# A two-layer decoder trunk on one core: index work of the expert layers split along the up tiles, low parts moved to VectorE, modulation loads moved

## The chip, the cores and the metric

The kernel runs on one core of one Trainium2 chip. The metric is the device time in microseconds (us) of one execution, the median of several runs. The engines are TensorE (PE in the rows; its weight loads are PEld), VectorE (DVE), ScalarE (ACT), GpSimd (POOL) and SyncE (SP), whose queue starts nearly all DMA transfers. Each engine works through its own instructions in the order in which they stand.

## What is computed

One sequence of 256 tokens with 1024 features passes two layers. The first mixes tokens by retention, the second by sparse attention; each ends with a PEER expert layer. The reference, cut to the expert layer and the modulation:

```python
mod = (c_act @ ada_w[layer] + ada_b[layer])          # shift, scale and gate, twice
h = x * (1.0 + sc2) + sh2
q = (xc @ w_q).reshape(T, PEER_HEADS, 2, PEER_QDIM // 2)
s = jnp.einsum('thcd,hcnd->thcn', q, sub_keys)
sv, si = lax.top_k(s, PEER_TOPK)                     # 16 of 128, two halves, 8 heads
comb = (sv[:, :, 0, :, None] + sv[:, :, 1, None, :]).reshape(T, PEER_HEADS, 256)
cv, ci = lax.top_k(comb, PEER_TOPK)                  # the largest sums
i1 = jnp.take_along_axis(si[:, :, 0], ci // PEER_TOPK, axis=-1)
i2 = jnp.take_along_axis(si[:, :, 1], ci % PEER_TOPK, axis=-1)
w = jax.nn.softmax(cv, axis=-1)
u = u_tab[i1 * PEER_NKEYS + i2]
a = jax.nn.gelu(jnp.einsum('td,thkd->thk', xc, u)) * w
y = jnp.einsum('thk,thkd->td', a, v_tab[i1 * PEER_NKEYS + i2])
```

The kernel does not gather experts. It computes all 16384 products with `u_tab`, multiplies them by a weight matrix W that is zero except at the chosen experts, and multiplies the result with all of `v_tab`.

## The kernel before

**Split numbers.** A float32 matmul is made of three faster ones (`mm3`, lines 120 to 122): both operands are split into a high part and the remainder, the low part. A loaded weight tile `raw` (128x1024, 512 KB, five buffers) is split in two halves of 128x512: ACT copies the high part (`hi`, line 96), and DVE or POOL subtracts for the low part (`lo`, line 103); four buffers each. In `split(raw, lo)` a letter per half names the engine: "d" is DVE, "p" is POOL. Activations are split likewise by `modulate`: ACT scales into `tmp` (line 165), DVE copies `hh` (line 98), DVE or POOL subtracts `hl` (line 103).

**Order.** PE runs in the order of the program text (`manual_schedule`). The other engines are ordered by a scheduler that keeps dependences and may pull an instruction ahead, except inside blocks marked with `WORKERS`.

**First stage** (retention's queries and keys). For each of eight slabs k, `prepare` multiplies two tiles of modulation weights with the conditioning row on DVE (line 301), forms the coefficients (lines 305, 306) and modulates `xT`; then two tiles `ret_qk` are split and 48 matmuls run. The block is marked, so all engines follow the text.

**Background modulation.** `ada_steps` is a generator: one step loads a tile of modulation weights, the next multiplies it on DVE with a row sum (line 140). `drain(bg, n)` takes n steps at chosen places: in the expert layers' loops, in `columns` and between the attention's units. A chunk is eight tiles, 16 steps.

**Expert layer** (`peer`, once per layer). After the queries, `first` takes the 16 largest of 128 for each head and half (lines 562 to 566). `second(tt)`, for each of two token tiles, builds 80 candidate sums (579 to 583), takes the 16 largest of each head (586 to 590), turns their places into two ranks (592 to 605) and looks up the indices by comparison and a tree of additions (608 to 613). Then 60 up tiles follow (`up`, 24 matmuls each, a gelu per pair at line 685). After up tile 15 `weights` takes the softmax (618 to 625), ahead of up tile 20, after tile 19, `finish` transposes indices and weights on PE, and from there `dense` builds W in 34 steps until tile 58 (`DENSE`, `UPLO` and `FINISH` hold these numbers; of the first half's tiles, 18 have their low parts on POOL). Then `down` tiles run, and the second half of experts repeats without index work. All of the index work is on DVE.

**Attention** (`nsa`). `columns` projects keys and queries tile by tile and takes three background steps ahead of each tile; `hidden` reads four `cmp_w1` tiles; `values` follows; then 16 units (`scores`, `turn`, `weighted`) of a head pair and a raw branch each, with two background steps in the first seven.

## Time and profile before

| | us |
|---|---|
| median of 3 runs | 2143.55 (2143.01 to 2144.36) |
| profiled execution, its time | 2146.44 |
| profiled execution, first to last instruction (span) | 2144.7 |
| PE, DVE, ACT, POOL busy | 2029.4, 1663.5, 1207.9, 315.4 |
| mean granted clock of TensorE, share of full | 0.977 |

All rows below are of the profiled execution, whose own time is 2.89 us above the median. Times in rows start at the first instruction. PE is busy for most of the span, so what is to be read are the stretches in which it is not, and the stretches in which its granted clock is under 1.00.

### The profile page before, as it was taken

How to read it: one execution, taken by the hardware profiler on the slowest of the kernel's cores; microseconds unless marked ns; L12 is line 12 of the kernel's file. 1: busy time of each engine (PE TensorE's matmuls, PEld its weight loads, DVE VectorE, ACT ScalarE, POOL GpSimd, SP SyncE). 2: the span in 40 equal slices, each digit the busy share in tenths (PEclk: the TensorE clock that was granted, in tenths of full speed). 3: DMA queues.
4: the chain of work that ended last, by engine and by line, in shares of the span. 5: the costliest groups of instructions: out<-in, count | busy, mean ns of one | idle time of the engine just before them, and what ended most of it. 6: DMA issues, size and time to landing. Idle time of an engine off the chain costs nothing.

```text
span 2144.7 us, 39749 instructions
## 1 busy us (share of the span) xinstructions
PE 2029.4 (95%) x14658; PEld 1820.6 (85%) x14658; DVE 1663.5 (78%) x3705; ACT 1207.9 (56%) x2141; POOL 315.4 (15%) x288
## 2 busy tenths in 40 slices
PE   6899996999999999999978999969999999999997
PEld 6788896999777999978868769969987889998885
DVE  7897589889876778886685766988897667779666
ACT  3455553666555666655542655546755556665554
POOL 3511485000000000000040237800000000000000
PEclk9999998999999999999989999989999999999999
DMA  8787553556777766786657426535567665556664
GB/s 302 244 296 235 187 162 122 161 158 187 232 228 236 220 207 206 219 251 216 195 175 266 168 70 187 160 119 163 165 208 228 188 185 165 166 170 213 194 187 138
DMA packets 116467, 417.06 MB, mean 194 GB/s; under 512 B 13072, under 2 KB 14640, under 8 KB 115376
## 3 DMA queue, kind: packets, MB, share of 16 engines
q1 hardware_dynamic: 115264, 411.90, 61.7%
q8 instruction: 114, 1.87, 0.4%
q10 hardware_dynamic: 1008, 2.63, 0.3%
q14 instruction: 81, 0.66, 0.1%
HBM read 411.31 MB, written 3.16 MB: 193 GB/s over the span
## 4 chain that ended last, share of the span: by engine, by line
PE 77%; DVE 14%; DMA 5%; issue 2%; POOL 1%; ACT 1%; SPq 0%; DVEq 0%; ACTq 0%; POOLq 0%
PE mm L120 12%; PE mm L122 12%; PE mm L121 12%; PE acc L122 11%; PE acc L121 11%; PE acc L120 11%; PE aux L664 3%; DVE lo L103 2%; DMA raw<-in_ada_w 2%; DVE big L612 1%; DVE raw L140 1%; ACT hi L96 1%; DVE big L610 1%; PE aux L982 1%; DMA raw<-in_kv_ada_w 1%
## 5 line engine op out<-in xcount | busy, mean ns | idle before, releaser
L96 ACT ACTIVATE hi<-raw 128x512 fp32r<-128x512 f32 x1272 | 797.0, 632 | 769.3 <-PE acc L122 345.2
L103 DVE TENSOR_TENSOR lo<-raw,hi 128x512 fp32r<-128x512 f32 x1108 | 772.8, 707 | 318.9 <-ACT hi L96 314.2
L120 PE MATMUL mm<-hh,hi 128*128 128x256 f32 x2528 | 730.7, 289 | 18.7 <-ACT hi L96 18.7
L122 PE MATMUL mm<-hh,lo 128*128 128x256 f32 x2528 | 718.1, 284 | 21.1 <-DVE lo L103 19.5
L121 PE MATMUL mm<-hl,hi 128*128 128x256 f32 x2528 | 715.4, 283 | 0.1
L122 PEld LDWEIGHTS mm<-hh,lo 128*128 128x128 f32 x2528 | 480.7, 190 | 24.3 <-DVE lo L103 20.9
L120 PEld LDWEIGHTS mm<-hh,hi 128*128 128x128 f32 x2528 | 481.7, 191 | 20.2 <-ACT hi L96 19.6
L121 PEld LDWEIGHTS mm<-hl,hi 128*128 128x128 f32 x2528 | 481.7, 191 | 1.1 <-POOL hl L103 0.3
L122 PE MATMUL acc<-hi,a 128*128 128x512 f32 x992 | 393.7, 397 | 3.7 <-DVE a L103 3.6
L121 PE MATMUL acc<-lo,a 128*128 128x512 f32 x992 | 392.9, 396 | 0.6 <-DVE lo L103 0.6
L120 PE MATMUL acc<-hi,a 128*128 128x512 f32 x992 | 392.3, 395 | 0.0
L103 POOL TENSOR_TENSOR lo<-raw,hi 128x512 fp32r<-128x512 f32 x164 | 228.4, 1409 | 920.2 <-ACT hi L96 914.4
L122 PEld LDWEIGHTS acc<-hi,a 128*128 128x128 f32 x992 | 186.4, 188 | 54.0 <-DVE a L103 9.1
L121 PEld LDWEIGHTS acc<-lo,a 128*128 128x128 f32 x992 | 186.4, 188 | 47.2 <-DVE lo L103 3.3
L120 PEld LDWEIGHTS acc<-hi,a 128*128 128x128 f32 x992 | 186.5, 188 | 43.4 <-issue 0.2
L140 DVE SCALAR_TENSOR_TENSOR raw<-raw,crow 128x1024 f32<-128x1024 f32 x96 | 121.5, 1270 | 58.7 <-DMA raw<-in_ada_w 46.8
L666 ACT ACTIVATE W<-aux 128x512 f32<-128x512 f32 x128 | 142.7, 1115 | 0.0
L269 POOL TENSOR_TENSOR x<-x,row 128x512 f32<-128x512 f32 x2 | 2.8, 1390 | 736.0 <-ACT x L268 736.0
L103 DVE TENSOR_TENSOR a<-g,a 128x256 fp32r<-128x256 f32 x248 | 103.7, 419 | 0.0
L96 ACT ACTIVATE a<-g 128x256 fp32r<-128x256 f32 x248 | 99.6, 403 | 1.8 <-DVE g L693 1.8
L693 DVE TENSOR_TENSOR g<-g,W 128x256 f32<-128x256 f32 x256 | 94.8, 422 | 1.0 <-ACT W L666 0.8
L655 DVE TENSOR_TENSOR hot<-iota,i 128x1024 f16<-128x1024 f16 x128 | 87.6, 685 | 0.0
(267 smaller groups left out, 1991.0 us busy)
## 6 DMA issues: line engine op xcount, KB each, us to landing
raw<-in_peer_u SPq DMA_DIRECT2D x256, 512.0 KB, 3.6
raw<-in_peer_v SPq DMA_DIRECT2D x256, 512.0 KB, 4.1
raw<-in_ada_w SPq DMA_DIRECT2D x96, 512.0 KB, 4.5
raw<-in_ret_in SPq DMA_DIRECT2D x32, 512.0 KB, 5.0
raw<-in_peer_q SPq DMA_DIRECT2D x32, 512.0 KB, 4.2
raw<-in_ret_qk SPq DMA_DIRECT2D x16, 512.0 KB, 5.8
raw<-in_ret_o SPq DMA_DIRECT2D x16, 512.0 KB, 3.7
raw<-in_kv_ada_w SPq DMA_DIRECT2D x16, 512.0 KB, 4.0
```

The lines of the kernel that those rows point to most:

```text
L96: nc.scalar.activation(dst, src, AF.Copy)
L103: (nc.vector if eng == "dve" else nc.gpsimd).tensor_tensor(dst, x, y, op=OP.subtract)
L120: nc.tensor.matmul(ps, sh, mh, start=start, stop=False, skip_group_check=True)
L121: nc.tensor.matmul(ps, sh, ml, start=False, stop=False, skip_group_check=True)
L122: nc.tensor.matmul(ps, sl, mh, start=False, stop=stop, skip_group_check=True)
L140: nc.vector.scalar_tensor_tensor(raw, raw, 1.0, crow, op0=OP.mult, op1=OP.mult, accum_out=mod[:, o + j:o + j + 1])
L610: V.tensor_tensor(o, o, sf[:, tt, c, :, None].to_broadcast([P, 16, 16, 8]), op=OP.mult)
L612: V.tensor_tensor(o[:, 0:n], o[:, 0:n], o[:, n:2 * n], op=OP.add)
L655: V.tensor_tensor(oA, count(0, P), bc(i2, P), op=OP.is_equal)
L664: nc.tensor.matmul(ps[:, t], ohA[n % 2][:, t], ohB[n % 2][:, x, t], start=(x == 0), stop=(x == 1))
L666: nc.scalar.activation(w[:, :, n * TB:n * TB + TB].rearrange("p b t -> p t b"), ps, AF.Copy, scale=1.0 / WSCALE)
L693: V.tensor_tensor(gi, gi, W[half][:, i % HALF], op=OP.mult)
```

## The change

Four edits, in one file. A constant is added ahead of everything, so a line of the changed kernel is one or more higher than the same line before (103 is 104, 966 is 985).

1. `second` ends after the largest sums. What followed is a generator, `ranks`, in 18 pieces for both token tiles, drawn between up tiles 5 and 18. `weights` comes after tile 9, its second part (`normalised`) after tile 19, `finish` after tile 20, `dense` from 21. Only eight up tiles have their low parts on POOL; from the ninth on they are DVE's.
2. In the first stage all low parts are DVE's; ACT makes the copy `hh`, but for slab 0.
3. `columns` takes no background steps. The attention's units take three steps each in the first eight and two in the next five.
4. One chunk of the second layer's modulation moves from the attention to the first expert layer's background; the down loop of the first half takes a step at each eighth tile more.

```diff
-UPLO = (["pp"] * 18 + ["dd"] * 42, ["dd"] * 60)
-DENSE = (20, 58), (0, 56)
-FINISH = (15, 19)
+UPLO = (["pp"] * 8 + ["dd"] * 52, ["dd"] * 60)
+DENSE = (21, 58), (0, 56)
+FINISH = (9, 20)
+RANKS = (5, 18)
...
-    def modulate(s, h, k, x, lo=None):
+    def modulate(s, h, k, x, lo=None, hi="dve"):
         nc.scalar.activation(t, x, AF.Identity, scale=cA[:, s, k:k + 1], bias=cB[:, s, k:k + 1])
-        copy_to("dve", h[0][:, k], t)
+        copy_to(hi, h[0][:, k], t)
...
-                modulate(0, h1, k, xT[:, k], "dve")
+                modulate(0, h1, k, xT[:, k], "dve", "act" if k else "dve")
...
-                            w[c] = split(load(a["ret_qk"][k, c]), lo="pd")
+                            w[c] = split(load(a["ret_qk"][k, c]), lo="dd")
...
+
+            def ranks(tt):
+
                 for c in range(2):
                     V.tensor_copy(sf[:, tt, c], si[:, tt, :, c].rearrange("p h j -> p j h"))
 
...
                 V.tensor_copy(r0, ci[:, tt].rearrange("p h k -> p k h"))
                 V.tensor_scalar(r0, r0, -1.0, 0.0, op0=OP.add, op1=OP.max)
                 V.tensor_scalar(q, p, 16.0, -8.0, op0=OP.is_ge, op1=OP.mult)
+                yield
                 V.scalar_tensor_tensor(r1, r0, -8.0, p, op0=OP.mult, op1=OP.add)
                 V.tensor_tensor(r1, r1, q, op=OP.add)
                 V.tensor_scalar(q, p, 72.0, None, op0=OP.is_lt)
                 V.tensor_tensor(r1, r1, q, op=OP.mult)
                 V.tensor_scalar(q, p, -72.0, 0.0, op0=OP.add, op1=OP.max)
                 V.tensor_tensor(r0, r0, q, op=OP.add)
+                yield
                 for c in range(2):
                     o = one[:, c]
                     V.tensor_tensor(o, iota8[:, :, None, :].to_broadcast([P, 16, 16, 8]),
                                     rr[:, tt, c, None].to_broadcast([P, 16, 16, 8]), op=OP.is_equal)
+                    yield
                     V.tensor_tensor(o, o, sf[:, tt, c, :, None].to_broadcast([P, 16, 16, 8]), op=OP.mult)
+                    yield
                     for n in (8, 4, 2):
                         V.tensor_tensor(o[:, 0:n], o[:, 0:n], o[:, n:2 * n], op=OP.add)
                     V.tensor_tensor(route[:, tt, 1 + c], o[:, 0], o[:, 1], op=OP.add)
+                    yield
 
             def weights():
                 w = route[:, :, 0]
...
+
+            def normalised():
+                w = route[:, :, 0]
...
+                ranking = (x for tt in range(2) for x in ranks(tt))
+                    if half == 0:
+                        lo, hi = RANKS
+                        due = lambda i: (min(max(i, lo), hi) - lo) * 18 // (hi - lo)
+                        drain(ranking, due(i + 1) - due(i))
+                    if half == 0 and i == FINISH[1] - 1:
+                        drain(ranking)
+                        normalised()
-                    if i % 2:
+                    if i % 2 or half == 0 and i % 8 == 0:
...
-                drain(bg, 3)
...
-                drain(bg, 2 if n < 7 else 10 ** 9)
+                drain(bg, 3 if n < 8 else 2 if n < 13 else 10 ** 9)
...
+        yield from ada_steps(a["ada_w"][1], 2, 64)
     def bg2():
-        for c in range(2, 5):
+        for c in range(3, 5):
```

DVE in an expert layer, from the second token tile's sums (579 to 583) on, before:

```order
L595 CAST big<-big 128x128
L583 TENSOR_TENSOR big<-big 128x8x8
L596 TENSOR_SCALAR big<-big 128x128
L599 TENSOR_SCALAR big<-big 128x128
L586 MAX big<-big 128x8
L597 CAST big<-big 128x128
L587 MAX_INDEX big<-big 128x8
L598 TENSOR_SCALAR big<-big 128x128
L588 MATCH_REPLACE big<-big 128x80
L600 SCALAR_TENSOR_TENSOR big<-big 128x128
```

and the changed kernel, at the end of the second tile's largest sums (591 is the last head's `max_index`, 600 to 610 are ranks, 614 and 617 the lookup):

```order
L591 MAX_INDEX big<-big 128x8
L602 TENSOR_SCALAR big<-big 128x128
L603 TENSOR_SCALAR big<-big 128x128
L104 TENSOR_TENSOR lo<-raw,hi 128x512
L605 SCALAR_TENSOR_TENSOR big<-big 128x128
L104 TENSOR_TENSOR lo<-raw,hi 128x512
L606 TENSOR_TENSOR big<-big 128x128
L104 TENSOR_TENSOR lo<-raw,hi 128x512
L607 TENSOR_SCALAR big<-big 128x128
L104 TENSOR_TENSOR lo<-raw,hi 128x512
L608 TENSOR_TENSOR big<-big 128x128
```

The first token tile's ranks stood among the second tile's largest sums; now they follow them, between the low parts of up tiles 8 and 9 (the `lo` rows).

SP's queue in the attention, from `columns` for the keys to the second `hidden`, before:

```order
L91 DMA raw<-in_nsa_k 128x1024
L91 DMA raw<-in_cmp_w 128x1024 x4
L91 DMA raw<-in_ada_w 128x1024 x2
L91 DMA raw<-in_nsa_q 128x1024
L91 DMA raw<-in_ada_w 128x1024
L91 DMA raw<-in_nsa_q 128x1024
L91 DMA raw<-in_cmp_w 128x1024 x4
L91 DMA raw<-in_ada_w 128x1024 x2
```

and of the changed kernel, from the keys to the output projection:

```order
L92 DMA raw<-in_nsa_k 128x1024
L92 DMA raw<-in_cmp_w 128x1024 x4
L92 DMA raw<-in_nsa_q 128x1024 x2
L92 DMA raw<-in_cmp_w 128x1024 x4
L92 DMA raw<-in_nsa_q 128x1024 x6
L92 DMA raw<-in_nsa_v 128x1024 x4
L92 DMA raw<-in_ada_w 128x1024 x16
```

The modulation tiles (`in_ada_w`) that stood between the weight tiles now stand behind all of them.

DVE at the attention's first units in the changed kernel (985 is the row maximum of the scores, 989 and 990 the softmax's scale, 1003 the copy of the transposed scores, 141 the multiplication of a modulation tile):

```order
L985 TENSOR_REDUCE m<-acc 128x1 x2
L1003 COPY pT<-aux 128x384
L989 RECIPROCAL sm<-sm 128x2
L141 SCALAR_TENSOR_TENSOR raw,mod<-raw,crow 128x1024
L990 TENSOR_TENSOR sm<-sm,gate 128x2
L989 RECIPROCAL sm<-sm 128x2
```

and before, at the first unit (966 is the row maximum, 970 and 971 the scale, 984 the copy, 156 a coefficient):

```order
L966 TENSOR_REDUCE m<-acc 128x1
L984 COPY pT<-aux 128x384
L970 RECIPROCAL sm<-sm 128x2
L156 SCALAR_TENSOR_TENSOR cB<-mod,cols 128x8
L103 TENSOR_TENSOR lo<-raw,hi 128x512
L971 TENSOR_TENSOR sm<-sm,gate 128x2
```

A modulation tile now stands inside each of the first eight units; before, all such tiles stood ahead of the first unit.

## Rows read from the trace of the kernel before

**Rows 1.** Page, part 1: busy time of each engine, share of the span, instructions.
```profile
PE 2029.4 (95%) x14658; PEld 1820.6 (85%) x14658; DVE 1663.5 (78%) x3705; ACT 1207.9 (56%) x2141; POOL 315.4 (15%) x288
```

**Rows 2.** Busy time by stretch: us, each engine (instructions), granted clock, DMA share, GB/s.
```profile
20.00:50.00 30.00, 25.54 (x200) 23.90 (x199) 26.02 (x42) 10.84 (x20) 11.97 (x8) 1.00 0.91 299
340.00:370.00 30.00, 13.36 (x100) 12.11 (x98) 29.73 (x95) 9.79 (x15) 11.48 (x7) 0.79 0.24 73
500.00:600.00 100.00, 99.02 (x534) 82.63 (x533) 87.19 (x188) 56.05 (x103) 0.00 (x0) 1.00 0.72 220
1100.00:1200.00 100.00, 86.71 (x611) 82.13 (x612) 68.86 (x122) 39.80 (x78) 19.25 (x16) 0.87 0.68 227
1380.00:1420.00 40.00, 23.22 (x172) 21.97 (x171) 38.89 (x104) 13.94 (x22) 18.24 (x11) 0.77 0.30 92
```

**Rows 3.** Timeline, PE, 352 to 378: start, length, operation [idle ahead <- releaser].
```profile
360.21 0.58 PE L120 MATMUL mm<-hh,hi 128*128 128x256 f32 x1 [7.11 <-ACT hi L96]
370.12 0.58 PE L122 MATMUL mm<-hh,lo 128*128 128x256 f32 x1 [9.11 <-DVE lo L103]
```

**Rows 4.** Timeline, ACT, 305 to 379: gelu of up pairs 2-3, 4-5 and 18-19.
```profile
312.23 0.58 ACT L685 ACTIVATE g<-mm 128x512 f32<-128x512 f32 x1
317.92 0.58 ACT L685 ACTIVATE g<-mm 128x512 f32<-128x512 f32 x1
...
378.29 0.58 ACT L685 ACTIVATE g<-mm 128x512 f32<-128x512 f32 x1
```

**Rows 5.** Timeline, DVE, 307 to 373: index work, and three low parts at its end.
```profile
308.93 0.60 DVE L580 TENSOR_TENSOR big<-big 128x448 f32<-128x448 f32 x1
...
311.99 0.38 DVE L586 MAX8 big<-big 128x8 f32<-128x80 f32 x2
...
318.99 0.62 DVE L592 CAST big<-big 128x128 f16<-128x128 uint32 x1
...
319.68 1.26 DVE L579 TENSOR_TENSOR big<-big 128x128 f32<-128x128 f32 x1
...
321.09 1.62 DVE L580 TENSOR_TENSOR big<-big 128x448 f32<-128x448 f32 x1
...
357.68 0.25 DVE L592 CAST big<-big 128x128 f16<-128x128 uint32 x1
...
368.36 0.29 DVE L613 TENSOR_TENSOR big<-big 128x128 f32<-128x128 f16 x1
...
370.38 1.89 DVE L103 TENSOR_TENSOR lo<-raw,hi 128x512 fp32r<-128x512 f32 x3
```

**Rows 6.** Timeline, POOL, 300 to 360: low parts of up tiles 4 to 17.
```profile
309.13 20.20 POOL L103 TENSOR_TENSOR lo<-raw,hi 128x512 fp32r<-128x512 f32 x15 [1.15 <-ACT hi L96]
329.49 21.99 POOL L103 TENSOR_TENSOR lo<-raw,hi 128x512 fp32r<-128x512 f32 x13 [0.16 <-ACT hi L96]
```

**Rows 7.** Timeline, DVE, 18 to 68: one period of the first stage.
```profile
20.43 1.21 DVE L301 SCALAR_TENSOR_TENSOR raw<-raw,crow 128x1024 f32<-128x1024 f32 x1
...
24.76 3.09 DVE L103 TENSOR_TENSOR lo<-raw,hi 128x512 fp32r<-128x512 f32 x2 [0.29 <-ACT hi L96]
27.78 1.21 DVE L301 SCALAR_TENSOR_TENSOR raw<-raw,crow 128x1024 f32<-128x1024 f32 x1
```

**Rows 8.** Page, part 5: a high part of 128x256 on ACT.
```profile
L96 ACT ACTIVATE a<-g 128x256 fp32r<-128x256 f32 x248 | 99.6, 403 | 1.8 <-DVE g L693 1.8
```

**Rows 9.** Timeline, DVE, 1090 to 1165: a modulation tile ahead of the attention.
```profile
1100.23 1.23 DVE L140 SCALAR_TENSOR_TENSOR raw<-raw,crow 128x1024 f32<-128x1024 f32 x1 [3.55 <-DMA raw<-in_ada_w]
```

**Rows 10.** Timeline, PE, 1086 to 1165: two waits in the attention's first part.
```profile
1096.02 3.75 PE L252 MATMUL acc<-ident,x 128*128 128x128 f32 x16 [7.34 <-DVE mv L226]
...
1161.74 0.39 PE L120 MATMUL mm<-hh,hi 128*128 128x256 f32 x1 [2.33 <-ACT hi L96]
```

**Rows 11.** Busy time by stretch, as rows 2: after a PE wait, and three attention units.
```profile
1095.00:1105.00 10.00, 6.78 (x28) 5.89 (x29) 6.16 (x18) 5.41 (x10) 2.47 (x5) 0.50 0.89 312
1225.00:1235.00 10.00, 10.00 (x84) 6.62 (x84) 7.21 (x31) 6.93 (x30) 5.20 (x14) 1.00 0.00 0
```

## The prediction

> **What bounds the kernel now.** I read the busy times first, then stretches, then the waits inside them. PE is busy for 2029.4 of 2144.7 us [rows 1], so the end is set by PE's work and by the places where PE stands still. In the two expert layers PE is busy for 13.36 of 30 and 23.22 of 40 us while DVE works almost without a pause, 29.73 and 38.89 [rows 2]: some 17 us of standing still in each. In the attention's first part it is busy for 86.71 of 100 us at a granted clock of 0.87, and in the first stage for 25.54 of 30 with DVE at 26.02 and DMA at 0.91 [rows 2].
>
> In the first expert layer the two waits are 7.11 and 9.11 us, ended by a high part on ACT and a low part on DVE [rows 3]. Both hang on the same thing: DVE has the whole index work ahead of the softmax and of its first low part. The price of it is best taken from the gelus, since the clock is in them too: a pair of up tiles takes 317.92 - 312.23 = 5.69 us when nothing is late, and from the second to the tenth pair it took 66.06 instead of 8 x 5.69 = 45.5 us [rows 4]. So **20.5 us** are lost there, 16.2 in the two waits and the rest at a low clock. The second layer repeats the pattern [rows 2].
>
> Why the index work is so long: while POOL subtracts low parts, DVE operations with two inputs in SBUF stretch. The same 128x448 addition took 0.60 and 1.62 us, and the second token's ranks and lookup, with POOL idle, ran from 357.68 to 368.6 [rows 5]. The searches for maxima do not stretch: eight heads took 311.99 to 318.99, 7.0 us [rows 5].
>
> **The change, part by part.**
>
> *Expert layers.* Removed from the path: 20.5 us. What is late next is the first low part that DVE makes, that of tile 8, since the order puts it behind all largest sums of the second token. Tile 8 would start at about 323.1 (the fourth pair's gelu is due at 312.23 + 2 x 5.69 = 323.6, and half a us lies between). POOL's part ends earlier: the fifteen operations from 309.13 are tiles 4 to 11, 1.35 each [rows 6], so the eighth, tile 7's second, ends at 319.9. From then on DVE runs at the short prices. The second token's sums begin at 319.68 [rows 5]; from there: 0.3 for the first addition, 0.6 for the 128x448 one, 0.5 for two small ones, 7.0 for eight heads, 0.9 for four pieces of the ranks that the scheduler pulled ahead (the small ones estimated from the 0.25 at 357.68 with POOL idle [rows 5]), and 0.63 for the low part (1.89 for three [rows 5]). That is 9.9, so 329.6, and a **wait of 6.5 us** at tile 8. If all the additions and casts still cost what they cost beside POOL (1.62 for the large one, 1.26 for each of the others), it is 10.5; if the first addition is the only one that starts earlier, nothing is below 5.
>
> Then DVE has both tokens' ranks beside low parts until `finish`: 10.9 us less an estimated 1.0 for what else stands between those rows, so 9.9 for each, 19.8 for both, some 1.6 for the softmax (six small steps), less the 0.9 above: 20.5. Thirteen tiles of two low parts are 26 x 0.63 = 16.4. The sum, 36.9, is just PE's time for thirteen tiles, 13 x 2.85 = 37.0. With no slack, wherever a run of large steps stands ahead of a low part PE waits for it, most at tile 11, where eight lookup steps stand ahead (about 3.6 us, a third of one token's 9.9); against that stands a lead of up to two tiles (four buffers). I take 3.5, between 0 and 8, and 1 for a low clock behind the wait. So 6.5 + 3.5 + 1 = 11 of the 20.5 stay, and a layer gains **9.5** (2 to 15.5), both 19. The softmax's two table loads on ACT move from tile 16 to tile 10 and hide, since high parts run up to two tiles ahead. `dense` takes 34 steps in 37 tiles, not 38: PE has the same products, DVE a few hundredths more per tile; nothing.
>
> *First stage.* DVE's period per slab is 27.78 - 20.43 = 7.35, with two low parts in 3.09 [rows 7], beside POOL's. Four low parts without POOL are 4 x 0.63 = 2.5: 0.6 less per slab. The copy `hh` costs 0.40 on ACT [rows 8] and frees about as much on DVE, which waits for it; nothing. Seven periods give 4. But DMA is at 0.91 there [rows 2], and 0.91 x 7.35 / 6.75 = 0.99, so DMA may be last next; I take **-3**, between -7 (the rotations behind this stage also lose POOL's company) and 0.
>
> *Attention.* Ahead of it DVE stood 3.55 us for a modulation tile and multiplied for 1.23 [rows 9], with `xsh` queued behind, and PE behind that: 4.8 us on the path. In the next 100 us PE idles for 13.3 [rows 2]; the waits are like that of 2.33 at 1161.74 [rows 10], a high part whose weight tile stood behind modulation tiles in SP's queue. `cmp_w1` still comes in fours, and the first tiles still wait for DVE; I take half of the 10.7 that the first item has not counted, 5.2. Together -10, between 0 and -18.
> Given back in the units: a unit is 26 matmuls, of which 84 took 10 us [rows 11], so 3.1 us, with 2.2 of DVE. Eight units get a multiplication of 1.23 each: 3.45, over PE's 3.1 by 0.35, so 3 us; and it stands between the reciprocal and the gate product, on the way to the transposes. I take +5, between 0 and 8 x 1.23 = 9.8. Eight tiles less stand ahead of `columns`' end, and their DMA is covered there by idle queues. Net **-5**.
>
> *Moved background.* Eight tiles more in the first layer's down loops. Where such tiles run beside down tiles now, PE idles for 0.98 of 100 us [rows 2]: **+0.5**, at most 2.
>
> Sum: -19 - 3 - 5 + 0.5 = -26.5. From the profiled execution's 2146.4 that is 2119.9; it is 2.9 above the median, so 2117 for the median.
>
> **The rivals.**
> *DVE stays full.* From tile 8 to 20 DVE has 36.9 us of work for 37.0; should the small steps cost a few tenths more each among low parts (40 of them), or the wait at tile 8 be the contended 10.5, each layer keeps 16 to 18 of its 20.5. Gain in both 5 to 9, total about -14: 2130. For it: DVE's work is sized to the last us. Against: with POOL idle the row shows the short prices [rows 5].
> *The clock stays low.* After a PE wait of 7.34 us [rows 10] the granted clock was 0.50 for the ten us from 1095 [rows 11], the lower level, 1.2 GHz. Should the 6.5 us wait at tile 8 be followed by ten such us, 5 us more are lost per layer, less the 3.5 that PE would have waited for DVE anyway and the 1 in the sum: +1 to +4 per layer, so 2122. For it: these rows. Against: ten us with further waits in them hold the clock down, and behind tile 8 the up tiles follow closely. The Trainium skill, "TensorE: Matmul & The Clock Gate", part 1, says that the throttled state is the default and activity releases it. By that rule the wait costs once more behind itself, as in this rival.
> *Units bound by DVE.* The full 9.8 in the units, and only the 4.8 ahead of the attention gained: +5 there instead of -5, total -16.5: 2127.
> *Slower: low parts cost 1.5 on DVE by themselves.* In the first stage a low part on DVE takes 1.5 [rows 7]. If that is their own price in a run of them, not POOL's doing, 28 in the first stage and 52 between tiles 8 and 20 cost about 0.9 more each, 72 us, against 26.5 gained: over 2180. It decides from 26.5 / 80 = 0.33 more per low part, 0.96 us. For it: the row. Against: 0.63 with POOL idle [rows 5].
> *It does not do what it says.* The scheduler could put the ranks back ahead of the low parts; the order shows only four small pieces pulled ahead. That would be 2143.
>
> **How the numbers follow.** The forecast has 0.68, with 2106 to 2124 as its own range; DVE full 0.12, low clock 0.08, units 0.05, slower 0.04, nothing 0.03. The range leaves out 2 in 10: from 2102, where the attention and the first stage give most of their upper bounds, to 2132, past the first three rivals. About 0.2% is what a measurement here can tell from no change, 4.3 us: faster 0.92 (all but the last two and a little), same 0.04, slower 0.04.
>
> **What would show it.** In the profile of after: the two waits before tile 20 gone, and one of 5 to 8 us ahead of tile 8, ended by a low part on DVE; from the second to the tenth gelu 55 to 58 us; additions of the second token short from 320 on; first-stage periods of 6.6 to 7.0; no wait for `in_ada_w` ahead of the attention; units of 3.4 to 3.8 us in the first eight. Wrong it would be with low parts over 0.9 us where POOL is idle, with waits of more than 8 us in all between tiles 9 and 20, or with units over 4.3.

## The result and the profile after

| | us |
|---|---|
| before, median of 4 runs | 2143.38 |
| after, median of 4 runs | 2116.53 (2115.28 to 2124.59) |
| ratio | 0.9875, 95% interval 0.9857 to 0.9893 |
| after, profiled execution, its time and its span | 2117.31, 2115.5 |

The changed kernel is 26.85 us faster, 23 to 31 by the interval; 2117 was forecast. The line numbers of the changed kernel are higher by one (a low part is 104, a modulation tile's multiplication 141) and by 12 to 19 further down (the gelu is 697, the block scores 927). Its page, part 1, answers to [rows 1]:

```profile
PE 2030.2 (96%) x14658; PEld 1817.2 (86%) x14658; DVE 1636.5 (77%) x3754; ACT 1211.4 (57%) x2148; POOL 226.9 (11%) x232
```

In sum PE is as busy as before in a span 29 us shorter: standing still went, not work. Where it went is read from fixed points that both traces have: the gelus (64 in a layer), the transposes ahead of the attention, the first block scores. "At" is the time of the changed kernel less that of the kernel before at the same point; "step" is what the stretch up to it brought.

| fixed point | before | at | step | forecast |
|---|---|---|---|---|
| first gelu (first stage and retention) | 307.94 | -3.8 | -3.8 | -3 |
| 2nd to 10th gelu, first layer | 378.29 | -12.6 | -8.8 | -9.5 |
| 32nd to 33rd gelu (first half's down tiles) | 709.83 | -8.6 | +4.1 | +0.5 |
| transposes to first block scores | 1186.65 | -24.5 | -16.0 | -10 |
| units, to the second norm's transposes | 1289.95 | -20.0 | +4.5 | +5 |
| 2nd to 10th gelu, second layer | 1425.58 | -28.7 | -9.4 | -9.5 |
| last gelu | 1962.43 | -29.1 | -0.4 | 0 |

Small steps between these rows make up the rest. The profiled execution of before was 3.06 over the median here and that of after 0.78, so 29.13 between the two are 26.85 in the medians.

Gelus of pairs 2-3, 4-5 and 18-19 on ACT, start and length, as in [rows 4]: 57.24 us from the first of them to the last, before 66.06, and 45.5 if nothing were late. Below, "between the gelus" is this stretch, from the second to the tenth gelu of a layer.

```profile
308.44 0.58 ACT L697 ACTIVATE g<-mm 128x512 f32<-128x512 f32 x1
314.13 0.58 ACT L697 ACTIVATE g<-mm 128x512 f32<-128x512 f32 x1
...
365.68 0.58 ACT L697 ACTIVATE g<-mm 128x512 f32<-128x512 f32 x1
```

The two PE waits that answer to [rows 3], and busy time by stretch around them (us; PE, PEld, DVE, ACT, POOL each with instructions; granted clock, DMA share, GB/s):

```profile
325.74 0.58 PE L123 MATMUL mm<-hh,lo 128*128 128x256 f32 x1 [6.19 <-DVE lo L104]
...
337.78 0.39 PE L123 MATMUL mm<-hh,lo 128*128 128x256 f32 x1 [1.74 <-DVE lo L104]
```

```profile
318.00:328.00 10.00, 3.81 (x24) 3.61 (x23) 10.00 (x70) 1.61 (x3) 0.00 (x0) 0.71 0.10 34
328.00:338.00 10.00, 8.26 (x65) 8.06 (x64) 10.00 (x21) 5.76 (x9) 0.00 (x0) 0.94 0.46 150
338.00:348.00 10.00, 10.00 (x72) 10.00 (x72) 9.29 (x26) 5.07 (x8) 0.00 (x0) 0.83 0.48 159
348.00:358.00 10.00, 10.00 (x86) 10.00 (x85) 10.00 (x20) 5.33 (x10) 0.00 (x0) 1.00 0.60 170
```

The long waits are 6.19 us at tile 8 and 1.74 at tile 11, DVE is full or nearly so all through, and the granted clock is under 1.00 in each of the first three stretches. DVE's rows behind them, which answer to [rows 5]:

```profile
315.89 0.27 DVE L580 TENSOR_TENSOR big<-big 128x128 f32<-128x128 f32 x1
...
316.31 0.60 DVE L581 TENSOR_TENSOR big<-big 128x448 f32<-128x448 f32 x1
...
325.00 0.68 DVE L104 TENSOR_TENSOR lo<-raw,hi 128x512 fp32r<-128x512 f32 x1
...
328.81 2.36 DVE L614 TENSOR_TENSOR big<-iota,big 128x2048 f16<-128x2048 f16 x2
331.08 0.69 DVE L104 TENSOR_TENSOR lo<-raw,hi 128x512 fp32r<-128x512 f32 x1
```

With POOL idle the 128x448 addition (581) takes 0.60 and the 128x128 one (580) 0.27, and the first low part ends at 325.7, at the time that the working gave (329.6, less the 3.8 by which all is earlier). The two comparisons (614) stand ahead of tile 10's low parts (331.08 is the first of them).

In the attention the wait ahead of the transposes is 6.35 for 7.34 [rows 10], and the block scores follow 77 us later, not 93; the first of these rows is PE's transposes, the second its second block scores:

```profile
1087.49 3.31 PE L253 MATMUL acc<-ident,x 128*128 128x128 f32 x16 [6.35 <-DVE mv L227]
...
1164.79 3.07 PE L927 MATMUL aux<-kc,qT 128*128 128x32 f32 x16 [0.66 <-DVE sc L930]
```

### The profile page after: what moved, and what is told of

Its sections match the earlier page's. It is cut to its first block, busy times and chain, and to the rows that moved or that the text cites. A ratio compares the mean times of both kernels' runs of the same rounds, so it can differ in the third digit from the quotient of the medians.

```text
span 2115.5 us, 39714 instructions
## 1 busy us (share of the span) xinstructions
PE 2030.2 (96%) x14658; PEld 1817.2 (86%) x14658; DVE 1636.5 (77%) x3754; ACT 1211.4 (57%) x2148; POOL 226.9 (11%) x232
## 4 chain that ended last, share of the span: by engine, by line
PE 79%; DVE 12%; DMA 4%; issue 3%; ACT 2%; POOL 1%; DVEq 0%; SPq 0%; ACTq 0%; POOLq 0%
PE mm L121 13%; PE mm L123 13%; PE mm L122 13%; PE acc L123 11%; PE acc L122 11%; PE acc L121 11%; DVE lo L104 3%; DMA raw<-in_ada_w 3%; PE aux L676 3%; DVE raw L302 1%; PE aux L873 1%; ACT hi L97 1%; DVE raw L141 1%; DMA raw<-in_kv_ada_w 1%; PE aux L557 1%
## 5 line engine op out<-in xcount | busy, mean ns | idle before, releaser
L104 DVE TENSOR_TENSOR lo<-raw,hi 128x512 fp32r<-128x512 f32 x1164 | 796.4, 695 | 317.8 <-ACT hi L97 314.1
L104 POOL TENSOR_TENSOR lo<-raw,hi 128x512 fp32r<-128x512 f32 x108 | 141.1, 1321 | 894.2 <-ACT hi L97 891.1
```

The lines of the kernel that those rows point to most:

```text
L104: (nc.vector if eng == "dve" else nc.gpsimd).tensor_tensor(dst, x, y, op=OP.subtract)
```

## The experiments

Each median stands against runs of the kernel before on the same chip (its medians there 2143.95 to 2145.66).

**The parts alone.** Three kernels carry one part each: the expert layers, the first stage, the modulation.

> The kernel before with the expert-layer part of the change alone (largest sums first, ranks in pieces, eight up tiles on POOL, softmax after tile 9, transposes after tile 20); first stage and modulation are as before. Theory 'the parts add up': in the trace of the changed kernel the two expert layers came out 8.8 and 9.3 us shorter from the second to the tenth gelu of a layer, so this kernel alone should gain 18 us (about 2125), with 57.2 us from the second to the tenth gelu in both layers. Rival 'the parts need each other' (the shorter first stage or the moved modulation tiles change what arrives when the expert layer starts): a gain under 15 us, or 59 us and more between those gelus in one of the layers.

> The kernel before with the first stage's part alone (all low parts on VectorE, the copy hh on ScalarE). Theory 'DVE's period was the bound': period per slab 6.7 us instead of 7.34, seven times, and the first gelu of the first expert layer 3.8 us earlier than before; total 2139.6. Rival 'the gain is used up behind the stage' (the rotations and what follows wait for loads that come no earlier): the first gelu less than 2 us earlier, total 2142 to 2144.

> The kernel before with the modulation part alone (no background steps in the columns, three and two steps in the units, one chunk moved to the first expert layer with a step more at each eighth down tile). Theory 'three prices': the stretch of the first half's down tiles in the first layer 4.1 us longer than before, the stretch from the transposes ahead of the attention to its first block scores 16 us shorter, the units 4 us longer; in all about -7, so 2136. Rival 'the attention's part is mostly the low clock of this profile of before': the attention's stretch only 8 to 11 us shorter, and with the same two costs the total is 2141 to 2144.

Measured: 2125.04 (ratio 0.9898, 0.9876 to 0.9919), 2140.60 (0.9984, 0.9969 to 1.0000) and 2140.63 (0.9981, 0.9969 to 0.9992). The gains, 18.9, 3.4 and 3.3, add up to 25.6 of 26.85, within what the intervals leave. The expert part's gelus are 56.0 us apart in both layers. The first stage brings the first gelu 5.1 earlier; the three kernels without this edit differ there by 2.5 among themselves. The modulation part makes the down stretch 5.7 longer and the attention's stretch 15.8 shorter, with 4.7 given back in the units. The attention's stretch, unchanged in the two other kernels, took 90.8 and 87.1 us there (90.6 before, 74.7 after), so 12 to 16 us are the edit's and not that one execution's clock. The stretches are those of this part's first theory, but the total lies nearer the second's 2141 to 2144 than the first's 2136: it had been counted from the profiled execution of before, 3 us over the median. No part needs another, as far as these intervals can tell.

**The clock after the wait.**

```diff
+                    if half == 0 and i == 8:
+                        idle = bank("aux").rearrange("p (a s) -> p a s", s=P)
+                        for _ in range(26):
+                            nc.tensor.matmul(idle, identb, identb[:, None, :].to_broadcast([P, 4, P]), ...)
                     up(base + i, UPLO[half][i])
```

> The changed kernel with 26 matmuls of 128x512 that nothing reads put on PE ahead of up tile 8 in both layers, some 5.5 us of PE time that lies inside the 6.2 us for which PE waits there anyway. Theory 'part of what stays is the clock': the 161 matmuls from 318 to 348 were busy for 22 us where 86 of them take 10.0 at the full clock, so 3.3 us per layer are the low clock after the wait; with PE kept busy the second to tenth gelu take 54 us instead of 57.2, and the total is 2110 to 2112. Rival 'the wait itself is all': the low clock comes from something else that these matmuls don't touch; the gelus stay 57 us or more apart, total 2116 to 2118.

Measured: 2122.98 (0.9892, 0.9870 to 0.9915), with 58.81 us between the gelus. PE's rows, and the two stretches:

```profile
318.55 5.79 PE L755 MATMUL aux<-identb 128*128 128x512 bf16 x26
...
325.13 0.39 PE L123 MATMUL mm<-hh,lo 128*128 128x256 f32 x1 [0.56 <-DVE lo L104]
...
335.38 0.42 PE L123 MATMUL mm<-hh,lo 128*128 128x256 f32 x1 [4.29 <-DVE lo L104]
```

```profile
318.00:328.00 10.00, 9.44 (x58) 6.19 (x58) 10.00 (x67) 1.82 (x4) 0.00 (x0) 1.00 0.10 24
328.00:338.00 10.00, 5.71 (x40) 5.51 (x39) 10.00 (x22) 4.47 (x7) 0.00 (x0) 0.88 0.31 97
```

The clock stayed at 1.00 (0.71 in the changed kernel), the wait at tile 8 was 0.56, and yet the gelus are further apart: PE stood 4.29 us at tile 10's low part, and the low clock came behind that. Neither theory gave this. The rows show a side effect: the scheduler put two products and four additions of the lookup ahead of tile 10's low parts, where in the changed kernel they stand around them. So this run shows that the clock follows PE being busy and doesn't price it. The price is in the changed kernel's own rows: PE went on at 337.78, when tile 11's first low part was there, so what the clock had cost until then (1.7 us: 89 matmuls busy for 12.07, at 8.6 matmuls per us) would have been a longer wait, and 1.6 us behind it were lost. This is worked out from the rows; no run isolates it. The Trainium skill, "TensorE: Matmul & The Clock Gate", part 1, has activity as what releases the throttle; the rows agree (0.71 and 1.00). Against the changed kernel the two gelu stretches are 3.2 us longer together, and the down stretch 4.8: its 185.4 us are the longest of the kernels with the same steps there, so that part is not shown to be the edit's.

**The order on DVE.**

```diff
-RANKS = (5, 18)
+RANKS = (9, 19)
```

> The changed kernel with the 18 pieces of the ranks drawn between up tiles 9 and 19 instead of 5 and 18. Theory 'order on DVE': the largest sums end at tile 8, by when seven tiles' pieces are due at once and stand ahead of the low parts of tiles 10 and 11; drawn later, the wait of 1.74 us at tile 11 goes and the second to tenth gelu take 54 to 55.5 us instead of 57.2; total 2111 to 2113. Rival 'DVE is full': DVE's work up to the transposes is the same, so the wait turns up between tiles 12 and 20 instead; 57 us stay, total 2116 to 2118.

Measured: 2108.78 (0.9831, 0.9814 to 0.9847), 53.44 and 53.12 us between the gelus; total and gelus are a little below what the first theory expected. In each layer one PE wait is left up to tile 20:

```profile
325.78 0.58 PE L123 MATMUL mm<-hh,lo 128*128 128x256 f32 x1 [5.46 <-DVE lo L104]
```

```profile
318.00:328.00 10.00, 4.54 (x30) 4.34 (x29) 10.00 (x73) 1.75 (x3) 0.00 (x0) 0.76 0.13 48
328.00:338.00 10.00, 10.00 (x78) 10.00 (x77) 10.00 (x26) 6.13 (x10) 0.00 (x0) 0.90 0.54 190
338.00:348.00 10.00, 10.00 (x86) 10.00 (x84) 10.00 (x26) 6.50 (x11) 0.00 (x0) 1.00 0.61 171
```

The first theory holds in its mechanism. DVE had the time; in the changed kernel all nine pieces of the first token tile, but for one addition, stand ahead of tile 11's first low part. This run also prices the clock better than the one before it: with one wait alone, 53.44 less 45.5 and 5.46 leaves 2.5 us (2.2 in the second layer), and the granted clock is 1.00 again from 338 to 348, where the changed kernel, with its second wait, has 0.83.

**POOL's company.**

```diff
-UPLO = (["pp"] * 8 + ["dd"] * 52, ["dd"] * 60)
+UPLO = (["pp"] * 18 + ["dd"] * 42, ["dd"] * 60)
```

> The changed kernel with the low parts of the first 18 up tiles on POOL, as before the change, and all else as changed. Theory 'POOL's company': beside POOL every addition, product and comparison of the index work stretches by two or more, the 16-bit ones of 128x2048 too (1.22 alone, 2.5 or more beside POOL); no wait at tile 8, but DVE is done with the ranks only at 360 to 366, and PE waits 6 to 10 us at the transposes after tile 20; the second to tenth gelu take 56 to 60 us. Rival 'order alone': taking the low parts off DVE and the ranks in pieces are enough, the ranks don't stretch, DVE is done at about 347, and the second to tenth gelu take 46 to 49 us; total 2095 to 2100.

Measured: 2126.11 (0.9920, 0.9893 to 0.9947), 62.1 us between the gelus. DVE's 128x2048 steps (the first begins just ahead of POOL's next low part, the second and third run beside POOL, the last runs alone), that low part, and PE's longest wait:

```profile
330.93 1.23 DVE L614 TENSOR_TENSOR big<-iota,big 128x2048 f16<-128x2048 f16 x1
332.20 2.30 DVE L617 TENSOR_TENSOR big<-big 128x2048 f16<-128x2048 f16 x1
334.42 2.31 DVE L614 TENSOR_TENSOR big<-iota,big 128x2048 f16<-128x2048 f16 x1
...
353.40 1.22 DVE L614 TENSOR_TENSOR big<-iota,big 128x2048 f16<-128x2048 f16 x1
```

```profile
331.04 2.37 POOL L104 TENSOR_TENSOR lo<-raw,hi 128x512 fp32r<-128x512 f32 x1 [4.18 <-ACT hi L97]
```

```profile
362.48 0.58 PE L123 MATMUL mm<-hh,lo 128*128 128x256 f32 x1 [8.73 <-DVE lo L104]
```

1.22 alone, 2.30 beside POOL, in 16 bits too. The first, 1.23, is not stretched; POOL's low part, which began 0.11 us behind it, took 2.37, where those before it, with DVE at the searches, take about 1.3. The wait is at tile 18, DVE's first low part, not at the transposes; its size was expected, and the gelus are 2 us further apart than that. The Trainium skill, "SBUF — State Buffer", section "SBUF: two separate sides", says that a DVE operation with two inputs in SBUF and a POOL operation that reads SBUF take turns at one pair of ports; the rows agree, and the maxima's searches (one input) don't stretch: 0.22 to 0.25 over 80 values in this run, with POOL busy or idle.

**The moved modulation tiles.** Two kernels place the eight extra steps otherwise: as pairs among the same down tiles, and as pairs among the second half's up tiles.

```diff
-                    if i % 2 or half == 0 and i % 8 == 0:
-                        drain(bg, 1)
+                    if i % 2:
+                        drain(bg, 2 if half == 0 and i % 6 == 1 and 1 < i < 50 else 1)
```

> The changed kernel with the same number of background steps in the first half's down tiles of the first expert layer, taken otherwise: two steps at once (a multiplication and the next load) at eight odd tiles, so that every multiplication stands two down tiles behind its load; in the changed kernel the steps at each eighth tile put some of them one tile behind. Theory 'distance': DVE waits 2.5 to 3.7 us for a modulation tile where it comes one tile after its load, with low parts queued behind; at two tiles these waits are 1.2, and the stretch from the 32nd to the 33rd gelu falls from 180.5 (182 and 185 in the two other kernels with these steps) to 177 to 178. Rival 'rate': three or four tiles more in the stretch through five buffers are the cost, however they stand: 180 to 185 stays.

```diff
-                        drain(bg, 1)
+                        drain(bg, 2 if l == 0 and i % 6 == 1 and 1 < i < 50 else 1)
                     up(base + i, UPLO[half][i])
...
-                    if i % 2 or half == 0 and i % 8 == 0:
+                    if i % 2:
                         drain(bg, 1)
```

> The changed kernel without the steps at each eighth down tile; the eight steps are taken instead as pairs among the second half's up tiles of the first expert layer, which have one step at every second tile. Theory 'down tiles have no room, up tiles have': the stretch from the 32nd to the 33rd gelu returns to 176.2 to 176.6 (as in the kernels with 16 modulation tiles there), and from the 33rd to the 64th gelu it stays at 205.7 within 0.5; 4 to 6 us less than the changed kernel in all. Rival 'a tile costs wherever it stands': the up stretch gets 3 us longer or more.

Measured: 2114.78 (0.9864, 0.9848 to 0.9881) with a down stretch of 181.3, and 2113.69 (0.9859, 0.9839 to 0.9879) with 176.1. The up stretch of the latter took 207.8 us, 2.1 more than in the changed kernel; but kernels without extra steps there took 205.7 to 207.8 (the first stage's part alone 207.75), so a price of its four tiles is not shown, and it is hardly over 2 us. In all it is 2.8 us faster than the changed kernel, not 4 to 6. So the rate counts and not the distance, and up tiles are the cheaper place. DVE and PE in the changed kernel, and DVE in the first of these two:

```profile
571.84 1.22 DVE L141 SCALAR_TENSOR_TENSOR raw<-raw,crow 128x1024 f32<-128x1024 f32 x1 [2.50 <-DMA raw<-in_ada_w]
```

```profile
573.73 0.50 PE L122 MATMUL acc<-lo,a 128*128 128x512 f32 x1 [0.29 <-DVE lo L104]
574.67 0.50 PE L123 MATMUL acc<-hi,a 128*128 128x512 f32 x1 [0.43 <-DVE a L104]
```

```profile
570.47 1.23 DVE L141 SCALAR_TENSOR_TENSOR raw<-raw,crow 128x1024 f32<-128x1024 f32 x1 [2.93 <-DMA raw<-in_ada_w]
```

DVE waits 2.5 us for a modulation tile, with low parts and gated values queued behind, and PE waits for these. Of all kernels here, the six with 16 or 17 modulation tiles in this stretch took 175.5 to 176.6 us, and the eight with 19 took 180.4 to 185.4. The other four of the eight moved tiles went into the second half's down loop, 11 for 7, and cost nothing that shows: from the 64th gelu to the transposes of the attention before and after took 180.3 and 180.6 us.

**All of them among up tiles.** The ranks are late here too. The attention's modulation tiles go to the first expert layer as well, one step at each odd up tile from 39 on, then two at each odd up tile of the second half.

```diff
-                    if half and i % 2:
-                        drain(bg, 1)
+                    if i % 2 and (half or l == 0 and i > 38):
+                        drain(bg, 2 if half and l == 0 else 1)
                     up(base + i, UPLO[half][i])
...
```

> The changed kernel with the ranks drawn between tiles 9 and 19, and all modulation tiles of the attention moved to the first expert layer: a step at each odd tile from 39 on of the first half's up tiles, at each odd down tile, and two steps at each odd tile of the second half's up tiles (30 modulation tiles there instead of 15). Theory 'up tiles have room': the attention from the first unit's transposes to the gate's is 4 us shorter than in the changed kernel, the first down stretch 176.2 to 176.6, and the stretch from the 33rd to the 64th gelu no more than 2 us longer; total 2099 to 2102. Rival 'rate': one load per 2.3 us through five buffers is what the down tiles could not take (one per 2.1 to 2.2 us); the up stretch gets 4 us longer or more, total 2104 to 2110.

Measured: 2129.26 (0.9931, 0.9915 to 0.9948). The down stretch is 176.5 and the units are 4 us shorter, as expected, but the up stretch is 25.8 us longer than in the changed kernel. DVE and PE there:

```profile
779.21 1.23 DVE L141 SCALAR_TENSOR_TENSOR raw<-raw,crow 128x1024 f32<-128x1024 f32 x1 [2.73 <-DMA raw<-in_kv_ada_w]
```

```profile
781.44 0.39 PE L123 MATMUL mm<-hh,lo 128*128 128x256 f32 x1 [1.46 <-DVE lo L104]
```

The second theory holds, with a price far above the 4 us it named: PE has 19 waits for DVE's low parts there, 18.7 us in all, where the changed kernel has none. Up tiles take four more modulation tiles for about 2 us at most, not fifteen more.

**What cost 16 us in the columns.**

```diff
+                for _ in range(1 + j % 2):
+                    V.scalar_tensor_tensor(spare, spare, 1.0, crow, op0=OP.mult, op1=OP.mult, accum_out=spare1)
                 proj(ps[:, j % 2], slab(w[j], j), act)
```

> The changed kernel with 18 multiplications of a resident 128x1024 tile on DVE among the columns, one or two ahead of each, as many as the modulation tiles there before, but with no load behind them (their result is not used). The change made the stretch from the transposes ahead of the attention to its first block scores 16 us shorter; this asks which half of a modulation tile cost that. Theory 'queue': the loads between weight tiles in SP's queue, and DVE waiting for them with low parts behind, were the price; the stretch stays within 4 us of the changed kernel's 74.7, total 2117 to 2121. Rival 'DVE time': 18 multiplications of 1.23 us are 22 us of DVE, and most of the 16 comes back; the stretch is 85 us or more, total 2126 or more.

Measured: 2124.58 (0.9903, 0.9886 to 0.9920); the stretch is 81.1 us, 6.4 longer than in the changed kernel. Between the two theories: DVE's time alone is 6.4 of the 16, and the loads and the waits for them should be the other 9.6, which no run isolated. What the traces show of them: in that stretch DVE stands 17.5 us for modulation tiles before, and 3.6 after. The scheduler put the first of these multiplications close together, ahead of and among the modulations, where they took 1.77 beside POOL's low parts, and 1.22 later:

```profile
1092.64 1.77 DVE L857 SCALAR_TENSOR_TENSOR spare<-spare,crow 128x1024 f32<-128x1024 f32 x1
...
1139.62 1.22 DVE L857 SCALAR_TENSOR_TENSOR spare<-spare,crow 128x1024 f32<-128x1024 f32 x1
```

**The copy in the first stage.**

```diff
-                modulate(0, h1, k, xT[:, k], "dve", "act" if k else "dve")
+                modulate(0, h1, k, xT[:, k], "dve")
```

> The changed kernel with the copy hh of the first stage back on DVE; only the low parts stay moved. Theory 'the copy is worth nothing': DVE waits for that copy anyway (1.12 us ahead of hl), so its 0.4 us are in the same chain on either engine; the period per slab stays 6.6 to 6.8 us, and the total 2115 to 2118. Rival 'the copy carries the gain': DVE is the bound of the period, which goes back to 7.0 or more, and the first gelu of the first expert layer comes 2.5 us later or more.

Measured: 2113.99 (0.9854, 0.9837 to 0.9870). Neither theory: the period is shorter, not the same. PE's waits, a period apart, before, in the changed kernel and here:

```profile
25.66 0.39 PE L122 MATMUL acc<-hh,lo 128*128 128x256 f32 x1 [0.90 <-POOL lo L103]
33.00 0.39 PE L122 MATMUL acc<-hh,lo 128*128 128x256 f32 x1 [0.90 <-POOL lo L103]
```

```profile
23.49 0.39 PE L121 MATMUL acc<-hh,hi 128*128 128x256 f32 x1 [0.23 <-ACT hi L97]
...
30.17 0.39 PE L121 MATMUL acc<-hh,hi 128*128 128x256 f32 x1 [0.23 <-ACT hi L97]
```

```profile
23.68 0.39 PE L123 MATMUL acc<-hh,lo 128*128 128x256 f32 x1 [0.36 <-DVE lo L104]
30.05 0.39 PE L123 MATMUL acc<-hh,lo 128*128 128x256 f32 x1 [0.36 <-DVE lo L104]
```

Busy time by stretch here, with the DMA share next to last; DVE's wait for the copy in the changed kernel; and DVE's four low parts here:

```profile
20.00:50.00 30.00, 28.19 (x227) 27.17 (x226) 26.49 (x59) 13.54 (x25) 0.00 (x0) 1.00 0.98 343
```

```profile
29.63 0.42 DVE L104 TENSOR_TENSOR hl<-tmp,hh 128x256 fp32r<-128x256 f32 x1 [1.12 <-ACT hh L97]
```

```profile
29.31 2.49 DVE L104 TENSOR_TENSOR lo<-raw,hi 128x512 fp32r<-128x512 f32 x4
```

The periods are 7.34, 6.68 and 6.37 us. Before, PE waited for a low part of POOL, and DVE 0.29 us for a high part ahead of its two low parts, 3.09 [rows 7]; here the four take 2.49 and this wait is gone. With the copy on ACT, PE waits for a high part and DVE 1.12 us for the copy, both in ACT's queue; here neither shows. The copy's move cost 0.31 per slab. The first gelu comes 7.5 us earlier than before.

**Put together.** Twelve up tiles on POOL, so that DVE's first low part is due after the largest sums; each piece of the ranks held behind the last low part ahead of it in the text, so that the scheduler can't pull it ahead of that; the extra steps among up tiles.

```diff
+UPLO = (["pp"] * 12 + ["dd"] * 48, ["dd"] * 60)
+DENSE = (24, 58), (0, 56)
+FINISH = (9, 23)
+RANKS = (12, 22)
...
+                        with tc.issue_after(state["lo"].ins):
                             drain(ranking, due(i + 1) - due(i))
```

> The changed kernel with three things: low parts of the first twelve up tiles on POOL instead of eight; the ranks drawn between tiles 12 and 22, each piece held behind the last low part that stands ahead of it in the text, with the transposes after tile 23; and the eight extra background steps among the second half's up tiles, as in the kernel before this one. Theory 'the wait at tile 8 is the order of the first low part': the additions beside POOL cost 4 us more (sums done at 328.9 on the time axis of the kernel with 18 tiles on POOL, not 324.8), but tile 12 is due only at 330.7, so no wait over 2 us, and the second to tenth gelu take 46 to 49 us (53.3 with the ranks late); total 2090 to 2096. Rival 'DVE is full to the transposes': the same work then ends in waits between tiles 13 and 24; the second to twelfth gelu, 65.4 with the ranks late, gain less than 3 us per layer, total 2099 to 2104.

Measured: **2099.67** (0.9790, 0.9774 to 0.9807), faster than both kernels. The gelus are 47.13 and 47.34 us apart, where 45.5 is nothing late, and this is all of PE's waits over 0.3 us up to tile 23:

```profile
341.94 0.39 PE L123 MATMUL mm<-hh,lo 128*128 128x256 f32 x1 [0.88 <-DVE lo L104]
...
358.74 0.39 PE L123 MATMUL mm<-hh,lo 128*128 128x256 f32 x1 [1.82 <-DVE lo L104]
```

```profile
318.00:348.00 30.00, 28.90 (x242) 28.49 (x241) 29.05 (x116) 17.73 (x28) 7.17 (x6) 1.00 0.57 164
```

The clock is 1.00 throughout. The waits and the gelus are those of the first theory, but the total is 3.7 us over its range and in that of the second: against the kernel before, the first half's later tiles, with `dense` in fewer of them, took 1.9 and 2.2 us longer, and the up stretch with the extra steps 2.5. The edits were not run one by one. The copy `hh` on DVE was not joined to them.

## Why the prediction was right, and where it was not

*Expert layers*, -19 forecast, -18.2 found. The removal and the wait at tile 8 were right in mechanism and size (6.5 forecast, 6.19 found). Its two smaller terms were mis-sized and cancel: 3.5 of further DVE waits were 1.74, and 1 for the low clock was 3.4 (the 161 matmuls from 318 to 348 are busy for 22.07 us; at 86 in 10.0, as in the ten us behind, they take 18.7). Half of that stands in for a DVE wait, as worked out above; behind one wait alone, with the ranks late, it was 2.5. That lookup steps ahead of tile 11 make PE wait there was right, and drawing them later removed it.

*First stage*, -3 forecast, -3.8 found (1.0 to 5.3 in the kernels with the same stage). Four low parts without POOL were worth 0.97 per slab, not 0.6: beside their shorter time, 2.49 for 3.09, DVE's wait of 0.29 for a high part went, which its row had shown [rows 7] and the sum left out; "the copy frees as much as it costs; nothing" was wrong by 0.31 the other way. DMA at 0.99 did not bind: at the shortest period it is at 0.98 and still PE's waits end on DVE.

*Attention*, -5 forecast, -11.5 found. The columns' part, -10, was -16, inside its bounds and far from the value taken. PE's first matmul of the columns and the busy time of the stretch, before and after:

```profile
1101.77 0.55 PE L120 MATMUL mm<-xsh,hi 128*128 128x256 f32 x1 [2.00 <-issue]
```

```profile
1096.02:1186.65 90.63, 77.77 (x570) 74.28 (x571) 60.73 (x100) 35.74 (x74) 19.25 (x16) 0.88 0.73 245
```

```profile
1090.55 0.36 PE L121 MATMUL mm<-xsh,hi 128*128 128x256 f32 x1
```

```profile
1087.49:1162.17 74.68, 70.44 (x571) 68.53 (x571) 41.54 (x66) 35.84 (x73) 17.37 (x16) 0.96 0.53 178
```

The first term, 4.8 for the modulation tile ahead, was 2.7: the first matmul followed the transposes' start by 5.75 us and now does by 3.06, since DVE's wait ran in part beside the transposes. The second, 5.2 of PE's idle time, was about 6.5: in the whole stretch the idle time fell from 12.9 to 4.2, some 2 of it with the first term. The rest was not in the sum: PE's busy time fell by 7.3 us for as many matmuls, at a granted clock of 0.96 for 0.88. How much of that is the edit's is open, since the first stage's part alone, with the columns as before, was busy for 73.9 there. The units' +5 was +4.5: the first eight follow each other every 3.84 us (3.39 before), just over the 3.4 to 3.8 that were named, and the last eight every 3.36 (3.23 before).

*Moved background*, +0.5 forecast, +4.1 found, over its bound of 2. This step failed. It took the idle time of a stretch with modulation tiles, 0.98 of 100 us, as what such tiles cost, and priced eight more by it; but the price is not per tile. Up to one modulation tile in four down tiles costs almost nothing: the first half's loop had 16 for 64, and its three more cost 4 to 9 us, while the four more in the second half's loop, 11 in all, cost nothing that shows.

So the median came out within 0.5 us by luck, in two places. A gain taken 6.5 too small and a loss taken 3.6 too small met, which leaves the traces 29.1 apart for the 26.5 forecast; and the profiled execution of after lay only 0.8 over its median, where the forecast took off 2.9. Single executions differ by more than that. Of the rivals, "the clock stays low" was half right in its rows (0.71, 0.94 and 0.83 behind the waits) and wrong in its price; "units bound by DVE" and "DVE stays full" did not come; the low part costs 0.68 on DVE by itself, not 1.5.

## What to carry to other kernels

Count what stands ahead of an engine's first urgent instruction, not only whether its work fits: the same DVE work in another order was worth 8 us in two layers, and with the first urgent instruction due later as well, and the ranks held behind it, the stretch lost 10 of its 57 us. A background load can be nearly free up to a rate and cost several us just past it (here past one tile in four), so a price per tile from below that rate is no price above it. Before giving a lower clock a price, look at which engine would be waited for at the full one.

## What the runs showed of the hardware

The DVE operations with two inputs in SBUF that were measured took 1.4 to 4.7 times as long beside POOL's subtractions, in 16 bits as in 32, and the small one the most: 128x2048 in 2.30 for 1.22, 128x448 in 1.62 for 0.60, 128x128 in 1.26 [rows 5] for 0.27, 128x1024 in 1.77 for 1.22. Searches for maxima over 80 values took 0.22 to 0.25 with POOL busy or idle. After a PE wait of 4.29 or 6.19 us matmuls came 0.21 us apart, later 0.12; with PE busy in that wait they came 0.12 apart at once. The first stage's DMA share rose from 0.91 to 0.98 and 343 GB/s as its period fell, without PE waiting for it.
